# Down projection, second pass: eleven K tile pairs in seven products, where it was nine pairs

## The chip, the cores and the metric

The kernel runs on one core of one Trainium2 chip. The metric is the device time of one execution in microseconds (us), lower is better. The core has a matrix engine (TensorE, PE in the profile; its weight loads are listed apart as PEld), a vector engine (VectorE, DVE), a scalar engine (ScalarE, ACT), GpSimd (POOL), SyncE (SP, which issues nearly all transfers here), and 16 DMA engines. Each engine works through a queue of its own in order, and waits for the others through semaphores.

## The reference

One encoder block over 256 tokens of width 2048, in float32: an input projection, a retention group and a latent attention group, an output projection with a layer norm, and a feed forward part:

```python
mix = jnp.concatenate([ret_out, mla_out], axis=-1) @ w_out[l]
x = _layer_norm(DEEPNORM_ALPHA * x + mix, ln1_g[l], ln1_b[l])
h = jnp.square(jax.nn.relu(x @ w_up[l])) @ w_down[l]
x = _layer_norm(DEEPNORM_ALPHA * x + h, ln2_g[l], ln2_b[l])
```

The change is inside the last product, `@ w_down`: 256 tokens by 8192 (K) by 2048 columns.

## The kernel before

**Number format.** Each float32 operand is split into two parts, `hi` (rounded to the format that PE reads, `fp32r`) and `lo` (the rest). One product of tiles is then three matmuls: hi by hi, hi by lo, lo by hi. The `hi` part of the weights is a cast on ACT (L389), the `lo` part a subtraction on DVE (L390).

**Down projection.** It runs in two passes `p` over the output columns, 1024 columns each. In a pass the 64 K tiles are taken as 32 pairs, in the order `pairs[p]`; the second pass takes pairs 28 to 31, 22 to 27, then 0, 1, 2 and so on up to 21. One pair is one job: one DMA of 1024 KB into a `raw` buffer (three buffers; a load is issued on SP and waits until the job three before has read its buffer for the last time), then its pieces on ACT and DVE, then its matmuls on PE. Outputs are four PSUM banks `d` (two token blocks by two halves of the columns).

A plain pair (`pair_products`) is eight products, 24 matmuls of 512 columns. It needs two pieces: `hi` and `lo` of each of its two K tiles, 128x1024 each.

A pair listed in `SEVEN[p]` is done as a two by two block product in seven products (`seven_products`, L1090): 21 matmuls. The two K tiles and the two token blocks (and column halves) are the blocks. Some of the products use sums of blocks, so more must be made on DVE and ACT ahead of it:

- token sums (`token_sums`, L364 to L369): four 128x128 operations, a cast on ACT (L368, `sx`), and a 128x512 subtraction (L369). For the pairs in `STORED` these were kept from the first pass and are not made again.
- weight sums (`weight_sums`, L400 to L402): one 128x1024 and two 128x512 operations, in the raw buffer and in the single tiles `t13` (shown as `t`) and `t4` (shown as `ut`).
- four pieces instead of two: `lo` of 128x1024 three times and of 128x512 once, and the same casts on ACT.

Four of the products go to further PSUM banks `s`, which `add_sums` adds to the residual after the last seven-product pair of the pass.

**What sets the order.** The program is written out by hand through jobs and pieces. Each group of matmuls is followed by `unit()`, which emits at most two further pieces. Converted pieces go into five slots `hi` and five slots `lo`; a piece is emitted only when the slot's former user is freed in program order, so the conversion runs at most five pieces ahead of PE:

```python
if job.slotted and job.emitted >= job.loose:
    if len(holders) >= NSLOT and not force and not holders[-NSLOT][0]:
        return False
```

The split of the activations (`r_split`, L1021 on ACT and L1022 on DVE, tile `rhl`, two buffers) is emitted once per two pairs between those pieces. The last four pairs (18 to 21) are staged, and used after the loop.

Of the kernel before, what the change touches and what calls it, by code (L numbers as in the profile page):

```python
# [34 lines left out]


ORDER = (tuple(range(16)), (14, 15, 11, 12, 13) + tuple(range(11)))
SEVEN = ((4, 7, 9, 12, 14, 17, 19, 22, 25, 27), (2, 4, 7, 9, 12, 14, 17, 19, 22))

STORED = (12, 9, 22, 25, 4, 7)  # L40

# [39 lines left out]
def kernel(  # L81
# [265 lines left out]
    def row_job(i, pieces):  # L347
        def load(job):
            norm_rows[i] = raw_tile(job, f"row{i}")
            nc.sync.dma_start(norm_rows[i], ln_rows[i:i + 1].partition_broadcast(P))  # L350
        other(load, pieces)
# [83 lines left out]
    def down_pair(p, pair, into=None, seven=None):  # L435
        def load(job):
            raw = raw_tile(job, f"raw_wd{p}_{pair}")
            nc.sync.dma_start(raw.rearrange("p (e c) -> p e c", e=2),
                              w_down[2 * pair:2 * pair + 2, :, p * 1024:(p + 1) * 1024].rearrange("e p c -> p e c"))

        def half(job, e, i, j):
            return job.raw[:, e * 1024 + i * P:e * 1024 + j * P]

        def sums():
            k = 2 * pair
            r0, r1 = (rr[k // 32][:, k % 32 + e] for e in range(2))
            st = spare_flat[:, seven * 512:(seven + 1) * 512].rearrange("p (i c) -> p i c", i=4)
            return token_sums(r0, r1, st, sums_of(seven, pair))

        def columns(job, t):  # L450
            return (job.raw.rearrange("p (e j c) -> p e j c", e=2, j=2)[:, :, 1],
                    job.raw[:, 0:1024].rearrange("p (j c) -> p j c", j=2), t.rearrange("p (j c) -> p j c", j=2))

        return weights_pair(f"wd{p}_{pair}", load, half, columns, None if seven is None or p == 1 and pair in STORED else sums, seven is not None, into)
# [4 lines left out]
    def sums_of(q, pair):  # L459
        q = 2 + STORED.index(pair) if pair in STORED else q  # L460
        return sums_view(extra["sx"][:, q * 1024:(q + 1) * 1024])
# [14 lines left out]
    for p in range(2):  # L476
        for n, pair in enumerate(pairs[p]):
            if p == 0 or n < 32 - NHELD:
                j_down[p][pair] = down_pair(p, pair, None, SEVEN[p].index(n) % 2 if n in SEVEN[p] else None)
                if p == 1 and n == STAGE_AT:  # L480
                    pair = pairs[1][32 - NHELD]
                    j_down[1][pair] = down_pair(1, pair, (2, 3))
            elif n > 32 - NHELD:
                j_down[p][pair] = down_pair(p, pair, (1, None) if n == 33 - NHELD else None)
    j_down[0][pairs[0][SEVEN[0][0]]].held = True
    row_job(2, [])
# [528 lines left out]
    def r_split(b, keep=None):  # L1015
        if keep is None:
            t = work.tile([P, 4, 512], F32R, tag="big", name="rhl", bufs=2)
        else:
            t = extra["sx"][:, (keep + 1) * 2048:(keep + 2) * 2048].rearrange("p (k t) -> p k t", k=4)
        r = rr[b // 8][:, b % 8 * 4:b % 8 * 4 + 4]  # L1020
        nc.scalar.copy(t[:, :, 0:S], r)  # L1021
        nc.vector.tensor_sub(t[:, :, S:], r, t[:, :, 0:S].bitcast(F32))  # L1022
        rhls[b] = t
# [54 lines left out]
    def seven_products(job, x, k, sums, cb, mb, first, last):  # L1078
        for a, w, o, pb, alone in ((("x", 1, 0), 0, 0, cb[0][0], False), (("s", 3), 0, 512, cb[0][1], False),
                                   (("x", 0, 0), 1, 0, mb[0], True), (("s", 1), 1, 512, mb[1], True),  # L1080
                                   (("s", 0), 2, 0, mb[2], True), (("s", 2), 2, 512, mb[3], True),
                                   (("x", 1, 1), 3, 0, cb[1][0], False)):
            use(job, w + 1)
            if a[0] == "x":
                h, l = (x[:, k + a[1], i * S + a[2] * P:i * S + (a[2] + 1) * P] for i in range(2))
            else:
                h, l = (sums[:, a[1], i] for i in range(2))
            hi, lo = job.hi[w][:, o:o + 512], job.lo[w][:, o:o + 512]
            for x_part, w_part, fst, lst in ((h, hi, True, False), (h, lo, False, False), (l, hi, False, True)):
                nc.tensor.matmul(pb, x_part, w_part, start=alone and first and fst, stop=alone and last and lst)  # L1090
            if o or w == 3:
                free(job, (w,))
                unit()
# [74 lines left out]
    extra["sx"] = slab.tile([P, 8192], F32R, tag="slab", name="sx")  # L1168
    j_down[0][pairs[0][SEVEN[0][0]]].held = False
    st2 = [stat.tile([P, 4, 6], F32, tag=f"ln{tb}", name=f"lm{tb}", bufs=1) for tb in range(2)]  # L1170
# [45 lines left out]
    for p in range(2):  # L1216
        cb = [[(acc, bank)[p](f"d{p}{tb}{j}") for j in range(2)] for tb in range(2)]
        mb = None
        for n, pair in enumerate(pairs[p][:32 if p == 0 else 32 - NHELD]):
            b = pair // 2  # L1220
            if n % 2 == 0:
# [5 lines left out]
                if p == 1 and n == STAGE_AT:  # L1227
                    r_split(ORDER[1][15], -1)
            if n in SEVEN[p]:
                if mb is None:  # L1230
                    mb = [(bank, acc)[p](f"s{p}{j}") for j in range(4)]
                seven_products(j_down[p][pair], rhls[b], pair % 2 * 2, sums_of(SEVEN[p].index(n) % 2, pair), cb, mb,
                               n == SEVEN[p][0], n == SEVEN[p][-1])
                if n == SEVEN[p][-1]:
# [154 lines left out]
```

## Time and profile before

| | us |
|---|---|
| median of three runs | 1112.53 |
| lowest and highest run | 1112.09, 1113.03 |
| span of the profiled execution | 1110.6 |
| median less span | 1.9 |

The profiled execution has no listed time of its own apart from its span, from the first to the last instruction. The 1.9 us between its span and the median of the runs is what lies around a span, as far as these numbers tell.

In the profile, rows of a timeline give the start in us, the duration, the engine, the line, the operation with output <- inputs, and a count; a bracket gives the idle time of the engine before the row and what ended it. Rows of several equal instructions in a row are merged. A matmul row's duration (0.39 us) is longer than the distance to the next one, because matmuls are pipelined; distances of starts are what counts.

### The profile page before, as it was taken

Reading aid. Unit: us, or ns where it says so; the run is one execution under the profiler, and the core shown is the slowest. Engines: PE = TensorE matmul, PEld = TensorE weight load, DVE = VectorE, ACT = ScalarE, POOL = GpSimd, SP = SyncE. Lnnn points to the kernel's source line nnn. Section 1 sums busy time; section 2 is a strip of 40 time slices with the busy share of each in tenths; the row PEclk is TensorE's granted clock in tenths of the full one; section 3 lists DMA queues with packets and bytes.
Section 4 is the critical chain, followed back from the end, with each engine's and each line's share of the span. In section 5 each row is a group of like instructions: output and inputs, shape, how many; then the busy total and the mean of one; then the engine's idle time right before and its main releaser. Section 6 shows DMA issues by size and latency. Waiting matters only on the chain.

```text
span 1110.6 us, 13644 instructions
## 1 busy us (share of the span) xinstructions
PE 1102.9 (99%) x5193; PEld 921.7 (83%) x5193; DVE 901.0 (81%) x1198; ACT 613.8 (55%) x793; POOL 9.6 (1%) x18
## 2 busy tenths in 40 slices
PE   9999999999999999999999999999999999999997
PEld 8888888888888889888888888888888888888885
DVE  6676684666656777898998999899999998999886
ACT  4445664535453446455656656656666673665650
POOL 0000000000000000000000000000000000000000
PEclk9999999999999999999999999999999999999999
DMA  8655365444465554566656756755656665656672
GB/s 306 222 205 192 119 228 184 145 168 161 144 258 197 199 198 152 189 216 207 222 166 213 221 158 193 221 168 180 223 191 195 204 213 196 215 189 200 204 251 104
DMA packets 92561, 217.08 MB, mean 195 GB/s; under 512 B 4177, under 2 KB 62545, under 8 KB 84433
## 3 DMA queue, kind: packets, MB, share of 16 engines
q1 hardware_dynamic: 92064, 215.64, 57.7%
q8 instruction: 40, 0.66, 0.2%
q10 hardware_dynamic: 432, 0.59, 0.2%
q14 instruction: 25, 0.20, 0.1%
HBM read 214.12 MB, written 2.10 MB: 195 GB/s over the span
## 4 chain that ended last, share of the span: by engine, by line
PE 96%; DVE 2%; DMA 1%; issue 0%; ACT 0%; POOL 0%; DVEq 0%; ACTq 0%; POOLq 0%
PE d L302 20%; PE u L302 18%; PE r L302 16%; PE o L302 8%; PE v L1090 5%; PE m L302 5%; PE s L1090 4%; PE u L1090 4%; PE d L1090 3%; PE up L734 2%; PE pu L734 2%; PE ut L1137 1%; PE pv L302 1%; PE up L740 1%; PE pu L740 1%; PE pq L302 1%
## 5 line engine op out<-in xcount | busy, mean ns | idle before, releaser
L302 PE MATMUL d<-hi_wd,rhl 128*128 128x512 f32 x664 | 182.9, 390 | 0.0
L389 ACT CAST hi_wu<-raw_wu 128x1024 fp32r<-128x1024 f32 x112 | 118.1, 1058 | 116.6 <-DVE raw_wu L401 57.9
L389 ACT CAST hi_wd<-raw_wd 128x1024 fp32r<-128x1024 f32 x125 | 130.0, 1052 | 75.8 <-PE d L302 33.5
L390 DVE TENSOR_TENSOR lo_wd<-raw_wd,hi_wd 128x1024 fp32r<-128x1024 f32 x125 | 148.6, 1220 | 18.2 <-ACT hi_wd L389 17.4
L302 PE MATMUL u<-hi_wu,x1hl 128*128 128x512 f32 x576 | 162.7, 393 | 0.0
L390 DVE TENSOR_TENSOR lo_wu<-raw_wu,hi_wu 128x1024 fp32r<-128x1024 f32 x112 | 133.3, 1220 | 23.4 <-ACT hi_wu L389 22.6
L302 PE MATMUL r<-hi_ret,xhl 128*128 128x512 f32 x512 | 147.1, 397 | 0.0
L302 PEld LDWEIGHTS d<-hi_wd,rhl 128*128 128x128 f32 x664 | 124.3, 188 | 25.7
L302 PEld LDWEIGHTS u<-hi_wu,x1hl 128*128 128x128 f32 x576 | 106.4, 188 | 20.9
L302 PEld LDWEIGHTS r<-hi_ret,xhl 128*128 128x128 f32 x512 | 93.9, 188 | 18.2
L302 PE MATMUL d<-lo_wd,rhl 128*128 128x512 f32 x332 | 102.6, 389 | 0.1
L191 DVE TENSOR_TENSOR lo_ret<-raw_ret,hi_ret 128x1024 fp32r<-128x1024 f32 x64 | 75.7, 1220 | 23.9 <-ACT hi_ret L190 23.7
L302 PE MATMUL u<-lo_wu,x1hl 128*128 128x512 f32 x288 | 88.9, 390 | 0.0
L302 PE MATMUL r<-lo_ret,xhl 128*128 128x512 f32 x256 | 79.4, 391 | 0.0
L190 ACT CAST hi_ret<-raw_ret 128x1024 fp32r<-128x1024 f32 x64 | 64.9, 1051 | 16.4 <-PE r L302 12.2
L302 PEld LDWEIGHTS d<-lo_wd,rhl 128*128 128x128 f32 x332 | 62.2, 188 | 13.4 <-DVE lo_wd L390 0.6
L302 PEld LDWEIGHTS u<-lo_wu,x1hl 128*128 128x128 f32 x288 | 54.1, 188 | 11.4
L302 PE MATMUL o<-hi_wo,mix 128*128 128x512 f32 x208 | 57.1, 392 | 0.0
L302 PEld LDWEIGHTS r<-lo_ret,xhl 128*128 128x128 f32 x256 | 48.1, 188 | 10.4
L191 DVE TENSOR_TENSOR lo_wo<-raw_wo,hi_wo 128x1024 fp32r<-128x1024 f32 x26 | 31.2, 1222 | 19.6 <-ACT hi_wo L190 18.9
L302 PEld LDWEIGHTS o<-hi_wo,mix 128*128 128x128 f32 x208 | 38.7, 188 | 7.8
L302 PE MATMUL m<-hi_mla,xhl 128*128 128x512 f32 (+1 forms) x168 | 42.5, 363 | 0.0
(297 smaller groups left out, 1908.6 us busy)
## 6 DMA issues: line engine op xcount, KB each, us to landing
raw_wu<-in_w_up SPq DMA_DIRECT2D x64, 1024.0 KB, 5.7
raw_wd<-in_w_down SPq DMA_DIRECT2D x64, 1024.0 KB, 5.5
raw_ret<-in_w_ret SPq DMA_DIRECT2D x32, 1024.0 KB, 4.8
raw_wo<-in_w_out SPq DMA_DIRECT2D x16, 1024.0 KB, 4.8
raw_mla<-in_w_mla SPq DMA_DIRECT2D x14, 672.0 KB, 4.7
raw_qk<-in_w_qk SPq DMA_DIRECT2D x8, 640.0 KB, 3.9
row<-in_ln_rows SPq DMA_DIRECT2D x4, 1024.0 KB, 4.7
raw_uv<-in_w_uv SPq DMA_DIRECT2D x2, 1024.0 KB, 4.7
```

The lines of the kernel that those rows point to most:

```text
L190: nc.scalar.copy(hi[:, o:e], r)
L191: nc.vector.tensor_sub(lo[:, o:e], r, hi[:, o:e].bitcast(F32))
L302: nc.tensor.matmul(accs[j][:, :w], x_part, w_part[:, a:a + w], start=first and fst and i == 0, stop=last and lst and i == len(steps) - 1)
L389: nc.scalar.copy(h, src)
L390: nc.vector.tensor_sub(l, src, h.bitcast(F32))
L734: nc.tensor.matmul(pb, hi[:, a:a + P], hl[:, k0 + i], start=first and i == ks[0], stop=last and i == ks[-1])
L740: nc.tensor.matmul(pb[:, 0:S], lo[:, a:a + P], hl[:, k0 + i, 0:S], start=False, stop=last and i == ks[-1])
L1090: nc.tensor.matmul(pb, x_part, w_part, start=alone and first and fst, stop=alone and last and lst)
L1137: nc.tensor.transpose(pts[i][:, f * P:(f + 1) * P], gathered[i][:, f * P:(f + 1) * P], ident)
```

## The change

`SEVEN[1]` gets two more entries, 11 and 21, so that eleven of the 28 pairs in the second pass's loop are done in seven products, where it was nine. The new entries are positions in the second pass; the pairs there are pair 1 and pair 11 (the order lists below and the tile names go by pairs: `wd_1`, `wd_11`). Neither is in `STORED`, so both make their token sums in this pass. Each stands directly before a pair that is done in seven products already: pair 2 (not stored) and pair 12 (stored).

```diff
-SEVEN = ((4, 7, 9, 12, 14, 17, 19, 22, 25, 27), (2, 4, 7, 9, 12, 14, 17, 19, 22))
+SEVEN = ((4, 7, 9, 12, 14, 17, 19, 22, 25, 27), (2, 4, 7, 9, 11, 12, 14, 17, 19, 21, 22))
```

On PE each of the two pairs loses three matmuls. On DVE ten rows are added for each, on ACT three, on SP and POOL none.

**First place, DVE, around pair 1** (`lo_wd_1_0` is the `lo` part of the first piece of pair 1, `rr` the activations, `xm` holds the raw sums, `sx` the converted ones). A piece of the difference, up to the second piece of the changed pair:

```order
-L390 TENSOR_TENSOR lo_wd_1_0_8073<-raw_wd_1_7979,hi_wd_1_0_8072 128x1024
-L390 TENSOR_TENSOR lo_wd_1_1_8083<-raw_wd_1_7979,hi_wd_1_1_8082 128x1024
+L364 TENSOR_TENSOR xm<-rr_3643 128x128
+L365 TENSOR_TENSOR xm<-xm,rr_3643 128x128
+L366 TENSOR_TENSOR xm<-rr_3643 128x128
+L367 TENSOR_TENSOR xm<-rr_3643,xm 128x128
+L400 TENSOR_TENSOR t_3672<-raw_wd_1_7979 128x1024
+L401 TENSOR_TENSOR raw_wd_1_7979<-raw_wd_1_7979,t_3672 128x512
+L402 TENSOR_TENSOR ut<-raw_wd_1_7979 128x512
+L369 TENSOR_TENSOR sx<-xm,sx 128x4x128
+L390 TENSOR_TENSOR lo_wd_1_0_8082<-raw_wd_1_7979,hi_wd_1_0_8081 128x1024
+L390 TENSOR_TENSOR lo_wd_1_1_8092<-raw_wd_1_7979,hi_wd_1_1_8091 128x1024
```

Eight operations now stand ahead of the first piece of pair 1. The third piece, the split of the activations (L1022) and the fourth piece follow; only then come the same eight operations for pair 2, and its first piece.

On ACT the same place before, the casts of pairs 1 and 2:

```order
L389 CAST hi_wd_1_0_8072<-raw_wd_1_7979 128x1024
L389 CAST hi_wd_1_1_8082<-raw_wd_1_7979 128x1024
L368 CAST sx<-xm 128x4x128
L389 CAST hi_wd_2_0_8100<-raw_wd_2_8048 128x1024
L1021 CAST rhl<-rr_3643 128x4x256
L389 CAST hi_wd_2_1_8119<-raw_wd_2_8048 128x1024
```

And on ACT in the changed kernel:

```order
L368 CAST sx<-xm 128x4x128
L389 CAST hi_wd_1_0_8081<-raw_wd_1_7979 128x1024
L389 CAST hi_wd_1_1_8091<-raw_wd_1_7979 128x1024
L389 CAST hi_wd_1_2_8098<-t_3672 128x1024
L1021 CAST rhl<-rr_3643 128x4x256
L389 CAST hi_wd_1_3_8117<-ut 128x512
L368 CAST sx<-xm 128x4x128
L389 CAST hi_wd_2_0_8144<-raw_wd_2_8048 128x1024
```

The split of the activations (L1021 on ACT, L1022 on DVE) has moved from behind the first piece of pair 2 to a place ahead of it, among the pieces of pair 1. The cast `hi_wd_2_0` stands behind the cast L368 of pair 2's token sums, which waits for DVE's L367.

**Second place, DVE, around pairs 11 and 12**, before:

```order
L390 TENSOR_TENSOR lo_wd_10_1_8454<-raw_wd_10_8362,hi_wd_10_1_8453 128x1024
L390 TENSOR_TENSOR lo_wd_11_0_8466<-raw_wd_11_8378,hi_wd_11_0_8465 128x1024
L390 TENSOR_TENSOR lo_wd_11_1_8476<-raw_wd_11_8378,hi_wd_11_1_8475 128x1024
L400 TENSOR_TENSOR t_3672<-raw_wd_12_8441 128x1024
L401 TENSOR_TENSOR raw_wd_12_8441<-raw_wd_12_8441,t_3672 128x512
L402 TENSOR_TENSOR ut<-raw_wd_12_8441 128x512
L390 TENSOR_TENSOR lo_wd_12_0_8488<-raw_wd_12_8441,hi_wd_12_0_8487 128x1024
L1022 TENSOR_TENSOR rhl<-rr_3643,rhl 128x4x256
```

The same stretch of DVE in the changed kernel, from behind the eight operations for pair 11 that now follow `lo_wd_10_1`:

```order
L390 TENSOR_TENSOR lo_wd_11_0_8489<-raw_wd_11_8392,hi_wd_11_0_8488 128x1024
L390 TENSOR_TENSOR lo_wd_11_1_8499<-raw_wd_11_8392,hi_wd_11_1_8498 128x1024
L390 TENSOR_TENSOR lo_wd_11_2_8506<-t_3672,hi_wd_11_2_8505 128x1024
L1022 TENSOR_TENSOR rhl<-rr_3643,rhl 128x4x256
L390 TENSOR_TENSOR lo_wd_11_3_8525<-ut,hi_wd_11_3_8524 128x512
L400 TENSOR_TENSOR t_3672<-raw_wd_12_8455 128x1024
L401 TENSOR_TENSOR raw_wd_12_8455<-raw_wd_12_8455,t_3672 128x512
L402 TENSOR_TENSOR ut<-raw_wd_12_8455 128x512
L390 TENSOR_TENSOR lo_wd_12_0_8546<-raw_wd_12_8455,hi_wd_12_0_8545 128x1024
```

Here too the split L1022 has moved ahead of the first piece of the pair that follows (pair 12), and two more pieces of pair 11 stand before that.

## The prediction

> **What bounds the kernel now.** First the page: which engine is busy, and what the chain that ended last consists of.
>
> ```profile
> PE 1102.9 (99%) x5193; PEld 921.7 (83%) x5193; DVE 901.0 (81%) x1198; ACT 613.8 (55%) x793; POOL 9.6 (1%) x18
> DVE  6676684666656777898998999899999998999886
> PE 96%; DVE 2%; DMA 1%; issue 0%; ACT 0%; POOL 0%; DVEq 0%; ACTq 0%; POOLq 0%
> ```
>
> PE bounds the kernel: 99% busy, 96% of the chain. Fewer matmuls should then mean less time. But in the last third DVE stands at 9 in nearly every slice. So, second, the busy time of each engine in stretches, around the first new pair (PE, PEld, DVE, ACT, POOL, clock):
>
> ```profile
> 980.00:1000.00 20.00, 20.00 (x90) 16.57 (x89) 19.67 (x24) 12.89 (x14) 0.00 (x0) 1.00 0.63 211
> 1000.00:1020.00 20.00, 20.00 (x90) 16.57 (x89) 19.75 (x20) 12.12 (x13) 0.00 (x0) 1.00 0.71 228
> 1102.00:1108.00 6.00, 2.41 (x5) 0.67 (x4) 4.90 (x10) 1.39 (x3) 1.14 (x2) 1.00 0.44 165
> ```
>
> From 980 to 1020 PE is full (20.00 of 20), and DVE as good as full too (19.67, 19.75). DVE bounds nothing only because it runs ahead of PE; work added to it has nowhere to go but into that lead. Third, the timeline of PE, for where each pair starts and what a pair costs:
>
> ```profile
> 979.48 0.39 PE L1090 MATMUL d<-hi_wd,rhl 128*128 128x512 f32 x1
> ...
> 984.24 0.62 PE L302 MATMUL d<-hi_wd,rhl 128*128 128x512 f32 x2
> ...
> 995.12 0.39 PE L1090 MATMUL d<-hi_wd,rhl 128*128 128x512 f32 x1
> ...
> 1046.80 0.39 PE L1090 MATMUL d<-hi_wd,rhl 128*128 128x512 f32 x1
> ...
> 1051.56 0.62 PE L302 MATMUL d<-hi_wd,rhl 128*128 128x512 f32 x2
> ...
> 1070.14 1.07 PE L302 MATMUL d<-hi_wd,rhl 128*128 128x512 f32 x4
> 1071.35 0.73 PE L302 MATMUL d<-lo_wd,rhl 128*128 128x512 f32 x2
> ```
>
> Pair 27 (seven products) runs from 979.48 to 984.24: 4.76 us for 21 matmuls, 0.227 each. Pairs 0 and 1 (plain) fill 984.24 to 995.12: 5.44 us each, so pair 1 starts at 989.68. Pair 2 starts at 995.12, pair 12 at 1046.80, pair 13 at 1051.56. All is dense but for one place: four matmuls from 1070.14 should hand over at 1071.05, and the next starts at 1071.35, a wait of 0.30 us.
>
> **What the change takes from PE.** Three matmuls per pair: 3 x 0.227 = 0.68 us, for two pairs **1.36 us**. That would be all of it if the operands were there in time.
>
> **What it adds to DVE, and where.** The timeline of DVE ahead of pairs 1 and 2:
>
> ```profile
> 970.60 2.54 DVE L390 TENSOR_TENSOR lo_wd<-raw_wd,hi_wd 128x1024 fp32r<-128x1024 f32 x2 [1.46 <-ACT hi_wd L389]
> ...
> 981.73 0.68 DVE L390 TENSOR_TENSOR lo_wd<-ut,hi_wd 128x512 fp32r<-128x512 f32 x1
> 982.33 4.62 DVE L390 TENSOR_TENSOR lo_wd<-raw_wd,hi_wd 128x1024 fp32r<-128x1024 f32 x4
> 986.87 0.28 DVE L364 TENSOR_TENSOR xm<-rr 128x128 f32<-128x128 f32 x1
> ...
> 987.80 1.22 DVE L400 TENSOR_TENSOR t<-raw_wd 128x1024 f32<-128x1024 f32 x1
> ...
> 990.39 0.68 DVE L369 TENSOR_TENSOR sx<-xm,sx 128x512 fp32r<-128x512 f32 x1
> 991.00 1.22 DVE L390 TENSOR_TENSOR lo_wd<-raw_wd,hi_wd 128x1024 fp32r<-128x1024 f32 x1
> 992.13 1.22 DVE L1022 TENSOR_TENSOR rhl<-rr,rhl 128x1024 fp32r<-128x1024 f32 x1
> 993.27 1.21 DVE L390 TENSOR_TENSOR lo_wd<-raw_wd,hi_wd 128x1024 fp32r<-128x1024 f32 x1
> ...
> 1022.28 2.54 DVE L390 TENSOR_TENSOR lo_wd<-raw_wd,hi_wd 128x1024 fp32r<-128x1024 f32 x2 [2.14 <-ACT hi_wd L389]
> ```
>
> The prices, from start to start: a 1024 piece (986.87 - 982.33) / 4 = 1.135; the 512 piece 982.33 - 981.73 = 0.60; the four token sums 0.93; L400 to L402 2.59; L369 0.61; the split L1022 1.14. A plain pair takes 2 x 1.135 = 2.27. The new form takes 0.93 + 2.59 + 0.61 + 3 x 1.135 + 0.60 = 8.14. So each new pair adds **5.87 us** of DVE to save 0.68 of PE.
>
> DVE last waits at 970.60 (1.46 us, for a free slot) and then works without a gap until past pair 2's pieces, so nothing absorbs the 5.87. At pair 1: its pieces are the last two of the four from 982.33, so DVE is done with pair 0 at 984.60. Then 4.13 for the eight new operations: `lo_wd_1_0` starts at 988.73 and is there at 989.95 (duration 1.22). PE wants it with its second matmul, 989.68 + 0.23 = 989.91: just in time, and the other pieces come every 1.135 for every 1.36 of PE. At pair 2, whose own eight operations come next:
>
> - before: `lo_wd_2_0` was ready at 991.00 + 1.22 = 992.22, wanted at 995.12 + 0.23 = 995.35: a lead of 3.1 us.
> - now it comes later by the 5.87 and by the L1022 that moved ahead of it, 1.14: at 999.23. It is wanted 0.68 earlier, at 994.67. **PE waits 4.56 us**; call it 4.6 with the hand-over between engines and the near miss of pair 1.
>
> From there pair 2's pieces keep ahead. At pair 4 DVE has 0.60 + 6 x 1.135 of pieces and splits and 2.59 of sums to make first: counted from `lo_wd_2_0` its first piece is there 10.0 us later, and PE gets there 10.2 us later. Then plain pairs refill the lead, and by pair 8 the slots are full again, as they were there before (the 2.14 us wait for a slot at 1022). So after the first place PE is late by 4.6 - 0.68 = **3.9 us**, and the second place begins with the old lead.
>
> **Second place, pairs 11 and 12**, on the clock of the old trace (all of it stands 3.9 later in the new one):
>
> ```profile
> 1032.71 1.06 ACT L389 CAST hi_wd<-raw_wd 128x1024 fp32r<-128x1024 f32 x1 [0.26 <-PE d L1090]
> ...
> 1048.12 1.22 DVE L390 TENSOR_TENSOR lo_wd<-raw_wd,hi_wd 128x1024 fp32r<-128x1024 f32 x1 [2.46 <-ACT hi_wd L389]
> ```
>
> The last piece of pair 10 is cast at 1032.71 (it waits for a slot from PE), so its `lo` starts at about 1033.8. From there slots no longer hold it up, since the sums that follow need none and give PE time to free some: 1033.8 + 1.135 for the piece, 4.13 of sums, three pieces, the L1022 (moved ahead again) and the 512 piece, 3 x 1.135 + 1.14 + 0.60, and pair 12's weight sums (stored, so 2.59 only) give 1046.8. `lo_wd_12_0` is ready at 1048.0. PE wants it at 1046.80 - 0.68 + 0.23 = 1046.35. **PE waits 1.7 us.**
>
> Net of the 0.68, pair 13 starts 1.0 us late on PE. DVE, which at the old 1046 to 1048 had 2.46 us of idle time, now runs through it: pair 12's other pieces (2 x 1.135 + 0.60), pair 13's first and the L1022 put pair 13's second piece at 1046.8 + 1.135 + 2.87 + 1.135 + 1.14 = 1053.1. The chain of waits shows where it stood before, and that from there the end hangs on it:
>
> ```profile
> 1050.40 1.23 DVE lo_wd L390
> 1051.63 0.02 issue
> 1051.65 5.66 DMA raw_wd<-in_w_down
> ...
> 1071.35 3.92 PE d L302 x16
> ```
>
> That piece started at 1050.40; it frees the raw buffer, the next load takes 5.66 us, its cast and a row of DVE work follow without slack, and the last of them ends the 0.30 us wait of PE at 1071.35. DVE is now 2.7 late there. PE is only 1.0 late, so **the wait at 1071 grows by 1.7 us**.
>
> **The sum.** -1.36 + 4.6 + 1.7 + 1.7 = +6.6 us. The span of 1110.6 becomes 1117.2. The median of the runs stood 1.9 above the span; the same on top gives **1119.1 us**, slower by 0.6%.
>
> **Costs put at nothing.** ACT has 3 more casts per new pair, at most 1.06 each by the row of 1032.71; ACT is busy 12.89 of 20 us, so it fits. But the cast of pair 2's first piece stands behind L368, which waits for DVE's L367: 988.73 + 3 x 1.135 + 1.14 + 0.60 + 0.93 = 994.8. Two casts later, at most 996.9, `hi_wd_2_0` is there, inside the wait above. SP and POOL get nothing new; a raw buffer freed by pair 1 at 992 lands at 998, pair 4 needs it at 1005. Two seven-product pairs in a row do not occur before; they share `t13` and `t4`. DVE works in order, so I take 0 for that; its bounds are 0 and one 0.61 row. The sums after the last pair and the tail keep their place behind pair 12.
>
> A standstill of PE in two pieces of some 2 us is not in the trace. The nearest row is the end, 1102 to 1108: PE idle for most of it, granted clock 1.00. By that row a standstill costs nothing more. If PE ran at half its rate for the whole of pair 2, that would cost 4.76 more. I take 0, by the nearest row, and keep part of the other end for the range. [...]
>
> **Rivals.** (1) *The lead holds*, not slower: PE only drops its 6 matmuls, 1112.53 - 1.36 = 1111.2, which is 0.12% less. For it: PE never waits for a piece before 1071. Against: it needs a lead of 7.7 us (5.87 + 1.14 + 0.68) at pair 2, and the rows give 3.1. It decides there: any lead under 7.7 is a stall. 5%. (2) *Only the first place stalls*: DVE makes good the second by the 2.46 and other waits: 1112.5 + 3.9 - 0.7 = 1115.7. Against: the idle time lies behind the point where pair 12 wants its piece. 9%. (3) *PE runs slower after the standstill*: up to 4.76 more by the bound above; at half of that, pair 2's second half at full rate again, 1121.5. Against: clock 1.00 in every row read. 9%. (4) *The scheduler leaves work away or the pairs don't change*: the order shows it all in place; 2%, 1112.5.
>
> **How the numbers follow.** Forecast 75%, with 1118.0 to 1120.2 of its own: 0.14 us per percent in the 14 us of work that DVE gets ahead of pairs 2 and 12, 0.6 for `t13`, 0.5 for the spread of the runs. The range goes part of the way to (2) and to (3): 1117.0 to 1121.0; it leaves out (1), (4), most of (2) and the upper part of (3), about 2 in 10. A measurement can tell about 0.2% (2.2 us) from no change. The whole gain is 0.12%, so even (1) is no change by that measure: with (4) and a share of (2) that makes same 7%, faster 1%, slower 92%.
>
> **What would show it.** PE should wait at pair 2 for `lo_wd` (two waits, some 2 us each, hi then lo), at pair 12 (1.7), and at 1074 to 1078 (2.0 in all, 0.30 before). DVE without a gap from 970.6 to past 1015; 1090-line matmuls up by 42, 302-line down by 48. If PE stays dense, the lead was read wrongly; if only the 1071 wait grows, the slots gave more than the rows show; if matmul distances after 999 are 0.45 instead of 0.227, it is (3).

## The result and the profile after

The changed kernel takes **1121.65 us** (median of five runs, 1120.73 to 1121.88); the kernel before, run beside it, 1112.98 (1112.09 to 1113.54). The ratio is 1.0079 with a 95% interval of 1.0067 to 1.0092: slower by 0.8%. The direction is as forecast; the time lies 2.5 us above the predicted 1119.1 and 0.65 above the upper end of the range. The profiled execution took 1121.76, its span is 1119.7, 9.1 more than before.

First the page of the changed kernel: busy time by engine, and the granted clock of PE in 40 slices.

```profile
PE 1104.9 (99%) x5187; PEld 921.4 (82%) x5187; DVE 911.9 (81%) x1218; ACT 617.6 (55%) x799; POOL 9.6 (1%) x18
PEclk9999999999999999999999999999999999989999
```

PE has 6 matmuls fewer (5193 before) and yet 2.0 us more of busy time (1102.9 before): some matmuls got longer. DVE has 10.9 us more. The 36th slice, where pair 2 is, has an 8 in the clock. The four longest rows of PE's waits (line, what it waited for, us in total, number, longest):

```profile
PE d L1090 <- DVE lo_wd L390: 3.8, 2, 2.2
PE d L1090 <- ACT hi_wd L389: 1.7, 1, 1.7
PE last L1292 <- ACT xm L1290: 1.5, 1, 1.5
PE d L302 <- DVE lo_wd L390: 1.0, 1, 1.0
```

Three rows of the four are new (the fourth grew out of the 0.30 us of before); the one at `last` was there before. The timeline of PE says where they are (start, duration, line, tiles, and in brackets the idle time before and who ended it):

```profile
984.43 0.62 PE L302 MATMUL d<-hi_wd,rhl 128*128 128x512 f32 x2
...
994.64 0.40 PE L1090 MATMUL d<-hi_wd,rhl 128*128 128x512 f32 x1
996.72 0.50 PE L1090 MATMUL d<-hi_wd,rhl 128*128 128x512 f32 x1 [1.69 <-ACT hi_wd L389]
999.45 0.80 PE L1090 MATMUL d<-lo_wd,rhl 128*128 128x512 f32 x1 [2.23 <-DVE lo_wd L390]
1000.04 0.63 PE L1090 MATMUL d<-hi_wd,rhl 128*128 128x512 f32 x1
...
1003.88 0.99 PE L1090 MATMUL s<-hi_wd,sx 128*128 128x512 f32 x2
1004.72 0.40 PE L1090 MATMUL s<-lo_wd,sx 128*128 128x512 f32 x1
...
1006.58 0.62 PE L302 MATMUL d<-hi_wd,rhl 128*128 128x512 f32 x2
...
1054.77 0.50 PE L1090 MATMUL d<-lo_wd,rhl 128*128 128x512 f32 x1 [1.56 <-DVE lo_wd L390]
...
1059.44 0.61 PE L302 MATMUL d<-hi_wd,rhl 128*128 128x512 f32 x2
...
1080.42 0.73 PE L302 MATMUL d<-lo_wd,rhl 128*128 128x512 f32 x2 [1.04 <-DVE lo_wd L390]
```

At pair 2 PE waits twice, 1.69 us for `hi` and 2.23 us for `lo`, with one matmul between. At pair 12 it waits 1.56, near the end 1.04. All three places were forecast, the last with 2.0 us. What was not in the forecast stands between 1000.04 and 1004.72: eleven matmuls in 4.68 us, 0.425 each, where 0.227 is usual. The windows of the changed kernel (start:end, length, then busy us of PE, PEld, DVE, ACT, POOL, then the granted clock) give the reason:

```profile
996.00:998.00 2.00, 0.50 (x1) 0.19 (x1) 1.93 (x4) 1.63 (x3) 0.00 (x0) 0.96 0.00 0
998.00:1000.00 2.00, 0.55 (x1) 0.50 (x2) 2.00 (x3) 2.00 (x4) 0.00 (x0) 0.50 0.00 0
1000.00:1002.00 2.00, 2.00 (x6) 1.57 (x5) 2.00 (x3) 1.47 (x3) 0.00 (x0) 0.50 0.13 20
1002.00:1004.00 2.00, 2.00 (x6) 1.52 (x6) 2.00 (x3) 1.03 (x1) 0.00 (x0) 0.50 0.92 287
1004.00:1006.00 2.00, 2.00 (x9) 1.60 (x8) 2.00 (x3) 1.05 (x1) 0.00 (x0) 0.83 0.54 221
1006.00:1008.00 2.00, 2.00 (x11) 1.63 (x10) 1.93 (x3) 0.36 (x1) 0.00 (x0) 1.00 0.64 106
```

The granted clock is 0.50 from about 998 to past 1004. In these windows a busy PE gets 6 matmuls into 2 us at 0.50 and 11 at 1.00: the second wait is followed by a stretch in which PE is counted as fully busy and does half the work. This is the third rival of the prediction, on top of the forecast and not in its place.

**The sum of the starts.** The same row of the program in both traces, with the distances from one to the next. Before, pair 0 started at 984.24, pair 3 at 995.12 + 4.76 = 999.88, pair 13 at 1051.56, and the last waiting row at 1071.35.

| stretch | before | after | difference | predicted |
|---|---|---|---|---|
| up to the start of pair 0 | 984.24 | 984.43 | +0.19 | 0 |
| pair 0 to pair 3 (first place) | 15.64 | 22.15 | +6.51 | +3.9 |
| pair 3 to pair 13 (second place) | 51.68 | 52.86 | +1.18 | +1.0 |
| pair 13 to the last waiting row | 19.79 | 20.98 | +1.19 | +1.7 |
| sum | | | +9.07 | +6.6 |

The terms of the second place and of the end are off by 0.2 and 0.5 us. The term of the first place is off by 2.6, and the slow matmuls account for nearly all of it: 4.68 - 11 x 0.227 = 2.18, and the longer step from 999.45 to 1000.04 (0.59 instead of the 0.34 that it takes at full clock in a run below) is 0.25 more: 2.43.

### The profile page after: what moved, and what is told of

The parts are those of the page before. It is cut to its first block, busy times and chain, and to the rows that moved or that the text cites. A ratio compares the mean times of both kernels' runs of the same rounds, so it can differ in the third digit from the quotient of the medians.

```text
span 1119.7 us, 13661 instructions
## 1 busy us (share of the span) xinstructions
PE 1104.9 (99%) x5187; PEld 921.4 (82%) x5187; DVE 911.9 (81%) x1218; ACT 617.6 (55%) x799; POOL 9.6 (1%) x18
## 4 chain that ended last, share of the span: by engine, by line
PE 93%; DVE 4%; DMA 1%; issue 0%; ACT 0%; POOL 0%; SPq 0%; DVEq 0%; ACTq 0%
PE d L302 19%; PE u L302 18%; PE r L302 16%; PE o L302 8%; PE v L1090 5%; PE m L302 5%; PE s L1090 4%; PE u L1090 4%; PE d L1090 3%; PE up L734 2%; PE pu L734 2%; DVE lo_wd L390 2%; PE ut L1137 1%; PE pv L302 1%; PE up L740 1%; DMA raw_mla<-in_w_mla 1%
## 5 line engine op out<-in xcount | busy, mean ns | idle before, releaser
L302 PE MATMUL d<-hi_wd,rhl 128*128 128x512 f32 x632 | 174.5, 390 | 0.0
L302 PEld LDWEIGHTS d<-hi_wd,rhl 128*128 128x128 f32 x632 | 118.3, 188 | 24.8 <-DVE rhl L1022 0.4
L302 PE MATMUL d<-lo_wd,rhl 128*128 128x512 f32 x316 | 97.8, 390 | 1.0 <-DVE lo_wd L390 1.0
L302 PEld LDWEIGHTS d<-lo_wd,rhl 128*128 128x128 f32 x316 | 59.2, 188 | 13.7 <-DVE lo_wd L390 1.5
L1090 PE MATMUL s<-hi_wd,sx 128*128 128x512 f32 x126 | 42.8, 394 | 0.0
```

The lines of the kernel that those rows point to most:

```text
L302: nc.tensor.matmul(accs[j][:, :w], x_part, w_part[:, a:a + w], start=first and fst and i == 0, stop=last and lst and i == len(steps) - 1)
```

## The experiments

In all of them lines are those of their own file, so L1090 can read L1091, L1096 or L1100. The kernel before was run beside each. Its median was 1112.96 beside the kernels with one new pair, with both waits filled and with the first filled, 1112.93 beside the one without all the sums of the new pairs, and 1112.78 beside the other four.

### One place at a time

Pair 1 alone:

```diff
-SEVEN = (..., (2, 4, 7, 9, 11, 12, 14, 17, 19, 21, 22))
+SEVEN = (..., (2, 4, 7, 9, 11, 12, 14, 17, 19, 22))
```

> Only pair 1 of the second pass takes the seven products, pair 11 stays at nine. Two theories of the 2.5 us by which the changed kernel is over the sum of the prediction. A, the slower clock: after the two waits at pair 2 PE runs at half rate for some 6.8 us, and that alone is the excess; then the first place costs the +6.5 us that its trace shows between the starts of pairs 0 and 3, again with a granted clock of 0.5, and the time is 1112.8 + 6.5 = 1119.3. B, the excess belongs to two new pairs together (the tail): pair 1 alone costs the predicted +3.9, 1116.7, with clock 1.00.

Measured: **1119.16 us**, ratio 1.0061 (1.0046 to 1.0076), which is A's 1119.3. Its waits at pair 2 are those of the changed kernel (1.67 and 2.23 us), and so is the clock behind them (windows of half a microsecond at the fall and the rise of the clock):

```profile
997.50:998.00 0.50, 0.00 (x0) 0.00 (x0) 0.50 (x1) 0.50 (x2) 0.00 (x0) 0.89 0.00 0
1004.50:1005.00 0.50, 0.50 (x3) 0.39 (x2) 0.50 (x1) 0.50 (x1) 0.00 (x0) 0.78 0.59 238
```

Pair 11 alone:

```diff
-SEVEN = (..., (2, 4, 7, 9, 11, 12, 14, 17, 19, 21, 22))
+SEVEN = (..., (2, 4, 7, 9, 12, 14, 17, 19, 21, 22))
```

> Only pair 11 takes the seven products, pair 1 stays at nine. By the prediction's steps the second place costs +1.0 at pair 12 and +1.7 at the wait before the last pairs, less 0.1 for what the trace of the change shows less: +2.4 to +2.7, 1115.2 to 1115.5, with one wait of about 1.6 us at pair 12 and a granted clock of 1.00 throughout, since no second wait follows. If a wait of 1.6 us is enough to lower the clock: half rate after it and 1117.5. If the second place stalls only because the first did: 1112.5.

Measured: **1115.22 us**, ratio 1.0023 (1.0013 to 1.0032), inside the 1115.2 to 1115.5. The waits of PE from 980 to 1090, and a window over pair 12's place (PE is idle in 1.57 us of it):

```profile
PE d L1090 <- DVE lo_wd L390: 1.6, 1, 1.6
PE d L302 <- DVE lo_wd L390: 1.0, 1, 1.0
```

```profile
1008.00:1060.00 52.00, 50.43 (x222) 41.42 (x222) 48.90 (x52) 31.95 (x35) 0.00 (x0) 1.00 0.60 200
```

The clock is 1.00: a wait of 1.6 us did not lower it here. The two places add up: +6.2 and +2.3 make 8.5, and both together cost 8.7. The excess over the prediction belongs to the first place; the second one, with the end that hangs on it, was priced at 2.7 and cost 2.3.

### The clock: the waits filled

Small matmuls of zeros (`warm`, 128x128, into a bank that is accumulated anyway) were put into the waits of pair 2. They change no other instruction.

```diff
-    def seven_products(job, x, k, sums, cb, mb, first, last):
+    def seven_products(job, x, k, sums, cb, mb, first, last, fill=(0, 0)):
+        def idle(n):
+            for _ in range(n):
+                nc.tensor.matmul(cb[1][0][:, 0:P], warm, warm, start=False, stop=False)
+        idle(fill[0])
...
                 nc.tensor.matmul(pb, x_part, w_part, start=alone and first and fst, stop=alone and last and lst)
+                if w == 0 and o == 0 and fst:
+                    idle(fill[1])
```

Three kernels: `fill` is (8, 10) at pair 2 for both waits, (8, 0) for the first alone, (0, 10) for the second alone.

Both waits:

> The changed kernel, with small matmuls of zeros added into an accumulator that PE would hold anyway, in the two waits of pair 2: 8 of them before its first product and 10 between its first product with hi and the one with lo. Nothing else is changed, and DVE and ACT deliver when they did. Theory A (standstill, then half clock): granted clock stays at 1.00, matmul distances stay 0.227 behind the wait, and the place costs +3.9 instead of +6.5: 1121.6 - 2.4 = 1119.2. Theory C (the wide distances behind the wait are waits for DVE's or ACT's pieces that only look like a slower clock): no change, 1121.6.

The first wait:

> As the kernel with both waits filled, but with only the 8 small matmuls ahead of pair 2's first product; the wait of about 2.2 us between hi and lo stays empty. If it takes both waits together (some 4 us with one matmul of 0.5 us between) to lower the clock: clock 1.00 and 1119.2. If the wait of 2.2 us is enough by itself: clock 0.5 and 1121.6, as in the changed kernel.

The second wait:

> The changed kernel with the 10 small matmuls of zeros in the second wait of pair 2 alone; the first of 1.7 us stays empty. The run with only the first wait filled still went to half clock, for a shorter time, after 2.2 us alone; pair 11's wait of 1.6 us did not. If the length of one wait decides and 1.7 us is below it: clock 1.00, pair 3 starts 2.5 us earlier than in the changed kernel, 1119.2 to 1119.6. If any wait of this size in this place does it: half clock for some 3.4 us, 1120.4.

| | changed kernel | both filled | first filled | second filled |
|---|---|---|---|---|
| idle left at pair 2, us | 1.69 and 2.23 | none | 2.22 | 1.69 |
| pair 0 to pair 3, us | 22.15 | 19.70 | 21.18 | 19.69 |
| time, us | 1121.65 | 1119.54 | 1119.32 | 1118.82 |
| ratio to before | 1.0079 | 1.0063 | 1.0059 | 1.0053 |
| its interval | 1.0067 to 1.0092 | 1.0048 to 1.0078 | 1.0042 to 1.0076 | 1.0038 to 1.0068 |

With the second wait filled (timeline of PE, and the window behind its second row):

```profile
996.43 0.50 PE L1096 MATMUL d<-hi_wd,rhl 128*128 128x512 f32 x1 [1.69 <-ACT hi_wd L389]
996.77 2.39 PE L1082 MATMUL d<-warm 128*128 128x128 f32 x20
999.16 0.50 PE L1096 MATMUL d<-lo_wd,rhl 128*128 128x512 f32 x1
999.50 0.40 PE L1096 MATMUL d<-hi_wd,rhl 128*128 128x512 f32 x1
999.73 0.39 PE L1096 MATMUL d<-hi_wd,sx 128*128 128x512 f32 x1
```

```profile
998.00:1000.00 2.00, 2.00 (x15) 1.68 (x14) 2.00 (x2) 2.00 (x3) 0.00 (x0) 1.00 0.00 0
```

The first `lo` matmul comes no earlier relative to pair 0 (999.16 - 984.13 = 15.03, in the changed kernel 999.45 - 984.43 = 15.02): the operand is late by as much. But the distances behind it are 0.23, the clock is 1.00, and pair 3 comes 2.46 us sooner. So the wide distances were the clock (theory A) and no waits for pieces (theory C), and **+4.05 of the first place's +6.51 is waiting, +2.46 is the slower clock**.

The times differ a little from what the place gives back. With both waits filled the time is 2.1 us less than that of the changed kernel, while the place gives back 2.45; the load in front of the last wait took 6.17 us there and 5.36 in the changed kernel. With the second filled it is 2.8 less, 0.4 below the expected stretch; its profiled execution had already reached pair 0 0.30 us earlier.

With the first wait filled and the second left, the median fits the first expectation (1119.2), but the profiled execution fits neither: it does go to half clock, but half as long as the changed kernel. Windows at the fall and the rise of the clock, of the changed kernel:

```profile
997.50:998.00 0.50, 0.00 (x0) 0.00 (x0) 0.50 (x2) 0.50 (x2) 0.00 (x0) 0.86 0.00 0
1004.50:1005.00 0.50, 0.50 (x4) 0.38 (x3) 0.50 (x2) 0.45 (x1) 0.00 (x0) 0.82 0.90 369
```

and of the kernel with the first wait filled:

```profile
999.00:999.50 0.50, 0.00 (x0) 0.00 (x0) 0.50 (x2) 0.50 (x2) 0.00 (x0) 0.87 0.00 0
1002.50:1003.00 0.50, 0.50 (x3) 0.36 (x3) 0.50 (x1) 0.50 (x1) 0.00 (x0) 0.72 0.47 180
```

The windows around these read 1.00 and 0.50, and tenths of a microsecond across the fall of the changed kernel read 1.00 up to 997.80, 0.79, and 0.50 from 997.90. So a clock of 0.86 over half a microsecond is full speed for 0.36 us and half speed for the other 0.14: the clock fell at 997.86 and rose at 1004.68, 6.82 us at half. With one wait left it fell at 999.37 and rose at 1002.78: 3.41 us, half of that. And only the profiled run of the four shows it in its mean clock (0.998, then 1.0, 1.0 and 1.0; their times are 1120.53, 1118.74, 1119.74 and 1118.90), where all five of the changed kernel have 0.996 or 0.997. The one wait of 2.2 us lowered the clock in one run of four, the two waits in all five.

### One wait instead of two

ScalarE's cast of pair 2's first piece is put ahead of its cast of pair 2's token sums, which waits for DVE:

```diff
         nc.scalar.copy(h, src)
+        if late.get(name):
+            late[name].pop()()
         nc.vector.tensor_sub(l, src, h.bitcast(F32))
```

(`late` holds the cast L368 and the subtraction L369 of pair 2's token sums; for pair 2 `token_sums` no longer issues them itself.)

> The changed kernel with ScalarE's cast of pair 2's first weight piece put ahead of its cast of pair 2's token sums, so that the first wait (1.7 us, put down to ScalarE) goes; VectorE's work and its order up to that piece are the same. Theory A (VectorE's queue is the bound): PE does the one hi matmul early and then waits about 4.3 us in one stretch for the lo piece; the start of pair 3 moves by less than 0.3 us, the clock is at half afterwards for as long or longer, 1121.3 to 1122.3. Rival (the ScalarE wait counts by itself): -1.7, 1119.9.

Measured: **1121.62 us**, ratio 1.0078 (1.0063 to 1.0093): theory A. The timeline of PE, and the windows where the clock falls and rises:

```profile
1000.04 0.52 PE L1100 MATMUL d<-lo_wd,rhl 128*128 128x512 f32 x1 [4.17 <-DVE lo_wd L398]
```

```profile
1000.00:1000.50 0.50, 0.46 (x2) 0.42 (x3) 0.50 (x1) 0.50 (x2) 0.00 (x0) 0.89 0.00 0
1003.50:1004.00 0.50, 0.50 (x3) 0.39 (x2) 0.50 (x2) 0.00 (x0) 0.00 (x0) 0.70 1.04 393
```

The wait put down to ScalarE is gone, and the one for VectorE is longer by as much as it and the matmul between them. It brought nothing: the wait for `hi` was the front part of the wait for `lo`. That the times agree so closely is in part luck, for two steps of theory A missed. Pair 3 was expected within 0.3 us of its old place, and the half clock to last as long or longer; in this execution it lasted from 1000.39 to 1003.80, 3.41 us, and pair 3 came at 1006.30 - 985.02 = 21.28 us behind pair 0, 0.87 less than in the changed kernel. The end got none of that: from pair 3 to pair 13 it is 52.87 as there, but the last stretch is 1080.59 - 1059.17 = 21.42, 0.44 longer, behind a load of 5.80 us (5.36 there), and pair 0 had started 0.6 later.

### VectorE's work taken away

```diff
-        return weights_pair(..., None if seven is None or p == 1 and pair in STORED else sums, ...)
+        return weights_pair(..., None if seven is None or p == 1 and pair in STORED + (1, 2) else sums, ...)
```

> The changed kernel without the token sums of pairs 1 and 2 of the second pass (their four sums on VectorE, the cast and the split; the products read what the tiles held). VectorE has 2 x (0.93 + 0.61) = 3.1 us less to do ahead of pair 2. If VectorE's work is what pair 2 waits for, its wait falls from 3.9 us to about 0.8 to 1.5, the granted clock stays at 1.00 (a wait of 1.6 us alone left it there), and with the second place and the tail as in the run with pair 11 alone (+2.3) the time is 1113.0 + 2.3 + 0.2 to 0.8 = 1115.5 to 1116.2. If pair 2 waited for ScalarE's casts or for slots instead, most of the wait and the time of 1121.6 stay; a part of it, with the clock still lowered, gives about 1119.

Measured: **1116.53 us**, ratio 1.0034 (1.0021 to 1.0046), 0.3 above the expected stretch. The timeline of PE, and the window behind it:

```profile
996.86 0.50 PE L1090 MATMUL d<-lo_wd,rhl 128*128 128x512 f32 x1 [1.38 <-DVE lo_wd L390]
```

```profile
998.00:1000.00 2.00, 2.00 (x11) 1.64 (x10) 2.00 (x3) 2.00 (x3) 0.00 (x0) 1.00 0.41 76
```

Taking 3.1 us from VectorE shortens the idle time at pair 2 from 3.92 to 1.38 and leaves the clock at 1.00: pair 0 to pair 3 takes 1001.53 - 984.90 = 16.63, +0.99 over before. 3.1 us of VectorE's work were worth 5.5 us of PE's time there, because they also carried the clock. The two casts of these sums on ScalarE (L368) are left out with them; the run before showed that moving ScalarE's cast out of the way brings nothing.

With all the sums of the two new pairs left out:

```diff
-            nc.vector.tensor_sub(t13, second, first)
-            nc.vector.tensor_sub(b12, b22, t1)
-            nc.vector.tensor_sub(t4, b21, b12)
+            if name not in ("wd1_1", "wd1_11"):
+                nc.vector.tensor_sub(t13, second, first)
+                nc.vector.tensor_sub(b12, b22, t1)
+                nc.vector.tensor_sub(t4, b21, b12)
...
-        return weights_pair(..., None if seven is None or p == 1 and pair in STORED else sums, ...)
+        return weights_pair(..., None if seven is None or p == 1 and pair in STORED + (1, 11) else sums, ...)
```

> The changed kernel without the token sums and weight sums of the two new pairs, 1 and 11 (their products read what the tiles held); all casts, splits and matmuls stay. VectorE's addition for a new pair falls from 5.87 us to 1.74. If VectorE's queue is the whole cause, the wait at pair 2 is 1.74 + 1.14 + 0.68 - 3.1 = 0.5 us or less, none stands at pair 12, the last wait is 0.3 to 0.5 us, the clock is 1.00, and PE's saving of 1.36 us shows for the first time: 1112.9 - 1.36 + 0.5 = 1112.0, bounds 1111.5 and 1112.6. If the seven products of the new pairs cost time by themselves (casts, slots, the order of PE): a time above 1113.5.

Measured: **1112.18 us**, against 1112.93 beside it; ratio 0.9991 (0.9982 to 1.0000). One wait is left from 980 to 1090:

```profile
994.48 0.50 PE L1091 MATMUL d<-lo_wd,rhl 128*128 128x512 f32 x1 [0.31 <-DVE lo_wd L390]
```

So without the sums (and the casts L368, left out with them) the new pairs cost no time. They are then about 0.1% faster, less than their 1.36 us, with an interval that reaches to no change. Pair 3 to pair 13 takes 1050.15 - 999.15 = 51.00, the full 0.68 less than before; at the first place the wait takes nearly all of it (999.15 - 983.58 = 15.57 against 15.64): listed with 0.31, it costs 0.6 from start to start, since the matmuls around it follow later than 0.227.

### The sums on GpSimd

GpSimd is idle in this stretch, so its queue was tried for the sums of the new pairs and of pair 2:

```diff
-            nc.vector.tensor_sub(t13, second, first)
...
+            eng = nc.gpsimd if name in ("wd1_1", "wd1_11") else nc.vector
+            eng.tensor_tensor(t13, second, first, op=ALU.subtract)
...
-            return token_sums(r0, r1, st, sums_of(seven, pair))
+            return token_sums(r0, r1, st, sums_of(seven, pair), nc.gpsimd if p == 1 and pair in (1, 2, 11) else None)
```

> The changed kernel with the token sums of pairs 1, 2 and 11 and the weight sums of pairs 1 and 11 on GpSimd instead of VectorE: 2 x 0.93 + 2.59 = 4.45 us less on VectorE ahead of pair 2, 0.93 + 2.59 = 3.52 less ahead of pair 12. If VectorE's work is the bound and GpSimd delivers in time without slowing it: waits at pairs 2 and 12 under 0.3 us, clock 1.00, 1111.5 to 1112.5, no slower than before. If GpSimd is slower than the 4.13 us that VectorE takes by enough to be late for pair 1's sums, or VectorE's rows lengthen while it works: part of the wait stays, 1114 to 1118. If GpSimd's sums are far late: above 1121.6. [...]

Measured: **1122.75 us**, ratio 1.0092 (1.0076 to 1.0107): no better than the changed kernel (1.0079, the intervals overlap), and above the 1114 to 1118 of the middle case. The timelines of GpSimd and of VectorE in this kernel:

```profile
980.93 3.31 POOL L401 TENSOR_TENSOR t<-raw_wd 128x1024 f32<-128x1024 f32 x1 [41.46 <-DVE lo_wd L390]
984.32 1.62 POOL L402 TENSOR_TENSOR raw_wd<-raw_wd,t 128x512 f32<-128x512 f32 x1
986.01 2.16 POOL L403 TENSOR_TENSOR ut<-raw_wd 128x512 f32<-128x512 f32 x1
```

```profile
981.90 2.89 DVE L390 TENSOR_TENSOR lo_wd<-ut,hi_wd 128x512 fp32r<-128x512 f32 x1
984.71 4.54 DVE L390 TENSOR_TENSOR lo_wd<-raw_wd,hi_wd 128x1024 fp32r<-128x1024 f32 x2
```

The three weight sums take 7.2 us on GpSimd (980.93 to 988.17), 2.6 on VectorE. While they run, VectorE's own rows stretch: 2.89 for a 512 piece that otherwise takes 0.68, 4.54 for two 1024 pieces that otherwise take 2.35. Those two rows alone give back 4.4 of the 4.45 us that VectorE was to be relieved of. PE waits earlier (0.73 and 1.01 us, at pairs 27 and 0) and again at pair 2, 3.10 us in one stretch, with half clock from 999.99 to 1003.40, 3.41 us. VectorE has no gap in this stretch, and it starts pair 2's first `lo` at 999.17, against 998.18 in the changed kernel, with 4.45 us less of its own to do. So it was the stretched rows that kept pair 2 waiting, and no late sum of GpSimd, as far as this trace tells. The 1024 row takes 3.31 us on GpSimd against 1.22 on VectorE, 2.7 times as long, beside a busy VectorE.

## Why the prediction was right, and where it was wrong

The direction and the places of the waits were right. The time lies outside the range because one term was put at nothing: what a standstill of PE costs beyond its own length.

**Right, by its own steps.** The first place: PE waits for pair 2's first piece, `hi` and then `lo`, as forecast; with the clock held up it costs +4.05 against the predicted +3.9. VectorE works there without a gap, as the prediction asked:

```profile
970.80 2.54 DVE L390 TENSOR_TENSOR lo_wd<-raw_wd,hi_wd 128x1024 fp32r<-128x1024 f32 x2 [1.46 <-ACT hi_wd L389]
...
1013.35 1.23 DVE L390 TENSOR_TENSOR lo_wd<-raw_wd,hi_wd 128x1024 fp32r<-128x1024 f32 x1 [1.08 <-ACT hi_wd L389]
...
1028.99 2.54 DVE L390 TENSOR_TENSOR lo_wd<-raw_wd,hi_wd 128x1024 fp32r<-128x1024 f32 x2 [2.14 <-ACT hi_wd L389]
```

One detail is early: the first gap is at 1013, not past 1015; PE's late start at pair 2 holds the slots. By 1029 VectorE waits 2.14 us for a slot again, as it did before at 1022: the lead is full, so the second place starts with the old one. There pair 12 waits 1.56 us (1.7 forecast). And the term at the end, which looked the least certain, is the old chain: the piece that frees the raw buffer, the load, the cast, VectorE's row of work. In the chain of waits of the changed kernel:

```profile
1059.86 1.15 DVE lo_wd L390
...
1061.02 5.36 DMA raw_wd<-in_w_down
...
1080.42 3.94 PE d L302 x16
```

The load starts 1061.02 - 1051.65 = 9.37 us later than before; less what was there by pair 3 (0.19 + 6.51) that is 2.67, against the predicted 2.7. PE was late by 1.18, and the load took 0.30 less: 2.67 - 1.18 - 0.30 = 1.19, the measured growth of that stretch (the wait itself grew from 0.30 to 1.04, where 2.0 was forecast). In the runs of this study that load took 5.2 to 6.2 us, which is where the end differs from kernel to kernel by some tenths.

Some of the agreement is luck. Without the clock's 2.46 us the span grew by 9.07 - 2.46 = 6.61, against a sum of 6.6; but +0.19 ahead of pair 0, +0.15 and +0.18 at the two places and -0.51 at the end cancel in it.

**Wrong: "By that row a standstill costs nothing more ... I take 0, by the nearest row."** That row, 1102 to 1108, was read as a standstill of 3.6 us with clock 1.00, and it outweighed the bound of 4.76. Measured, the standstill costs **2.46 us** more, about half of that bound, and without it the sum gives 1121.65 - 2.46 = 1119.2; the kernels with the clock held up came out at 1119.5 and 1118.8. So rival (3), given 9%, happened as well as the forecast; its price "at half of that" (2.4) was right, and its chance was not. The row also said less than it was taken for. It adds up two separate stretches of idle time (1.54 and 2.06 us), and it stops too early. The last two matmuls of the kernel before, and the window behind the one that was quoted:

```profile
1104.92 1.02 PE L1293 MATMUL last<-row,warm 128*128 128x512 f32 x2
```

```profile
1108.00:1110.00 2.00, 0.00 (x0) 0.00 (x0) 0.00 (x0) 0.00 (x0) 0.00 (x0) 0.77 0.47 160
```

PE is idle from 1105.94, and the clock does fall: a mean of 0.77 over 2 us, with 1.00 up to 1109.00 and 0.50 from 1109.50 on, is half speed from 1109.08 on, 3.14 us after the last matmul. So the trace of before shows one row further on that the clock fell once in a standstill; that two waits of some 2 us with a matmul between them are enough, it does not show.

**The rivals.** (1), the lead holds: refuted by the waits; the time comes near its 1111.2 only with the sums left out (1112.18). (2), only the first place stalls: refuted, pair 11 alone costs 2.3 us. (4): refuted by the counts of matmuls.

**Still open.** What exactly lowers the clock was not varied by itself. The profiled executions show this much of it:

| kernel | PE's waits at pair 2, us | clock falls at, us | rises at, us | at half clock, us |
|---|---|---|---|---|
| changed kernel | 1.69, one matmul, 2.23 | 997.86 | 1004.68 | 6.82 |
| pair 1 alone | 1.67, one matmul, 2.23 | 997.89 | 1004.72 | 6.83 |
| cast ahead | 4.17 | 1000.39 | 1003.80 | 3.41 |
| sums on GpSimd | 3.10 | 999.99 | 1003.40 | 3.41 |
| first wait filled | 2.22 | 999.37 | 1002.78 | 3.41 |
| second wait filled | 1.69 | 1.00 up to 1012 | | 0 |
| sums of pairs 1 and 2 left out | 1.38 | 1.00 up to 1012 | | 0 |

The two waits of the changed kernel, 3.92 us together, went with twice the time at half clock of the single one of 4.17. Nor does the clock fall at one point of a wait: in the changed kernel it fell 0.64 us into the second wait, which starts at 997.22, and with the cast ahead 0.35 us after the wait had ended at 1000.04. Why that is so, and why the single wait of 2.2 us lowered the clock in one run of four, was not shown.

## What to carry to other kernels

Fewer matmuls are worth something only where the engines that make their operands have that much lead; here 0.68 us of PE was bought with 5.87 us on an engine that was full, and its lead of 3.1 us was too small for it. Price a standstill of PE with the clock behind it, even if it is split by a matmul (here 1.69 and 2.23 us, and 2.46 us more for the clock), and look for a row in mid-kernel before you call that cost zero. When an operand is late anyway, small matmuls in the gap are worth a try: here they kept the clock at 1.00 and delayed nothing (15.03 us from pair 0 to the late operand's matmul, 15.02 without them), but they only give back the clock's share, 2.5 of the 8.7 us.

## What the runs showed of the hardware

- Two waits of 1.69 and 2.23 us with one matmul between them went with 6.82 us at half clock (changed kernel); one of 2.22 us with 3.41 us, in one run of four (first wait filled); one of 3.10 us (sums on GpSimd) and one of 4.17 us (cast ahead) with 3.41 us each. Three kernels with waits of 1.38 us (sums of pairs 1 and 2 left out), 1.57 us (pair 11 alone) and 1.69 us (second wait filled) stayed at 1.00 around them.
- At half clock eleven 512-column matmuls in a row stood 0.425 us apart (changed kernel, 1000.04 to 1004.72), at 1.00 the 21 of pair 27 0.227 (kernel before).
- 128x1024 float32 subtractions on VectorE, 1.2 us each, took about twice as long while GpSimd ran subtractions of the same kind (4.54 for two, against 2.35; sums on GpSimd); one of 128x512 took 2.89 instead of 0.68.
